# A hybrid recurrence and pooling decoder layer: heads by single levels among halves of projections, mean square in two fp32r passes, two meta queries directly, down projection in written order

## Chip, cores and metric

One core of a Trainium2 chip. The metric is the device time of one launch in microseconds (us). The engines are called PE (matrix unit), DVE (vector), ACT (scalar, activations), POOL (general purpose) and SP (which issues most transfers).

## The reference

One decoder layer over 1024 tokens of width 1024, with 16 learned meta tokens ahead of them, so L = 1040 rows, all in float32. Cut to what matters here:

```python
u = rmsnorm(h, mix_norm_pre)
q, f_logit, i_in, g_out, v_pool, gate_a, gate_b = split(u @ w_in)
a = hgrn2(q, f_logit, i_in, g_out, lb, out_gain)         # 4 heads of 128
p = multiscale_pool(v_pool, pool_proj, pool_scale)       # windows 2, 4, 8, 16
z = sigmoid(gate_a) * (a @ w_branch_hgrn) + sigmoid(gate_b) * (p @ w_branch_pool)
h = h + rmsnorm(z @ w_out, mix_norm_post)
u = rmsnorm(h, ffn_norm_pre)
gt = causal_dwconv(u @ ffn_w_gate, ffn_conv_w, ffn_conv_b)
y = (gelu(gt) * (u @ ffn_w_up)) @ ffn_w_down             # 2816 wide
h = h + rmsnorm(y, ffn_norm_post);  return h[:, N_META:]
```

Inside `hgrn2`, each head is a gated linear recurrence: with f = lb + (1 - lb) sigmoid(f_logit), b = cumsum(log f) and k = (1 - lb) sigmoid(-f_logit), the output at t is the sum over s <= t of (q_t exp(b_t - b_s) k_s) v_s. It is then divided by its root mean square over the 128 channels of the head, times a gain and sigmoid(g). Only the 1024 tokens leave the layer; of the 16 meta tokens the mixer needs outputs for the last two alone, since the convolution of width 3 looks two rows back.

## The kernel before

Everything lies with channels on the partitions and the 1040 rows along the free axis. A float32 product of full accuracy is made of three passes in fp32r, a rounded float32: each operand x is split into `xhi` (a cast by ACT) and `xlo` (the rest, by a subtraction), and hi*hi, hi*lo and lo*hi are added up in a bank of PSUM. A projection (`proj`) does this for 128 output channels: 8 blocks of k, three chunks of the rows (`CH_ALL`, 348 + 346 + 346 columns, or `CH_Q`, 3 x 342 for the last 1026 rows), one bank per chunk. The big products (gates, ffn, down projection) use Strassen's scheme.

The program runs through these stages (us of the profiled execution): projection of v up to 80; two early projections of the output gate g (heads 0 and 1, banks `pg`, made into `sg` by `post_g`) up to about 105, with the sums for the Strassen gates interleaved; the gates up to 250; the **head stage** from 250 to about 596; mixer output, ffn and, from about 1127, the down projection with its norm.

In the head stage the order is written in the string `ORDER`. A capital letter with a number is a projection for PE: F, Q, G for gate logit, query and output gate of a head, PV and PP for the pooling branch, BA and BB for the two branch products. `c` starts a head's chain on the logits (`chain_f`: clamps, logarithm, and the scan that gives b), `h2` is the next step of head 2, `sp`, `sa`, `w` are other small pieces. A scheduler then orders each engine's instructions from this program; so what stands on an engine follows from the written order and the scheduler's model.

A head's steps are the generator `head_steps`. The decayed scores within chunks of 128 are built by levels: for level lv = 2, 4, ..., 64 a block of 2 lv rows gives its second half's queries against its first half's keys, relative to the middle row. `level_in` makes `d`: a subtraction on b (L648), two exponentials on ACT, and the products with q (L652) and with kk (L653). `level_mm` multiplies on PE into `sl` (L668 with 64 columns, L664 for levels 32 and 64), and `level_out` copies the valid places into the score tile `sc`. Levels of 2, 4 and 8 also cover the meta tokens, with small matmuls into `sm` (L673) copied into `scm`. Then come the diagonal (`e1`, base, bank `sb`), the transposed keys `kt`, the sums of states over chunks (`ds`, added up by seven steps on DVE, L763), the outputs `po` from `sc` with v and from `qs` with the states (L780, L781; L773 for the meta rows), the square `rs` on ACT, and the mean square as a matmul with a matrix of 1/128 (`ms`, L788), plain fp32, one pass over three banks of 342 columns.

`POOLED` lists the operations that run on POOL instead of DVE: `sub` is the subtraction, `lq` and `lk` the products with q and kk, each with level and head; `w` a projection's weight split. `Loader` loads the weights of projections three ahead.

Steps of a head before, one per `h`: the inputs of levels 2 and 4; their matmuls and the inputs of 8 and 16; those and the inputs of 32 and 64; their matmuls, kd and e1; kt and base; ds; po and the square; ms.

The down projection runs in three stages of 11 steps (k). Each step's operands are loaded, cast (`rot`, L1496, ACT) and split (L1497, DVE) two steps ahead by `ahead`, and 24 matmuls into banks `pd` follow. For the last part, products `yh`, `yl` are prepared early from loads `yw` by `prep_last`.

Of the kernel before, what the change touches and what calls it, by code (L numbers as in the profile page):

```python
# [57 lines left out]
ORDER = ("F0 c0 Q0 h0 F1 h0 c1 Q1 h0 h1 F2 h1 c2 h0 Q2 h1 h2 G2 h0 h1 h2 h0 F3 h0 h2 c3 PV0 h1 h2 h1 Q3 h3 h1 h3 h1 "  # L58
         "PV1 h3 sp0 PV2 h2 h3 sa1 sp1 sp2 PP0 h2 PV3 h2 h3 sp3 PP1 h0 G3 w0 h3 PP2 h3 PP3 w1 BB0 w4 h2 BB1 w4 BB2 "
         "w4 sa2 BB3 w5 h3 BB4 w5 BB5 w5 sa0 sa3 BA0 BA1 w5 BB6 w2 BA2 w3 BB7 BA3 BA4 BA5 BA6 BA7")  # L60
POOLED = ("e1k.0 e1k.3 kdmul.2 kdmul.3 kdsub.2 lk32.1 lk4.1 lk64.0 lq16.1 lq16.3 lq32.0 lq32.1 lq32.2 lq4.0 "
          "lq64.0 lq64.3 lq8.0 lq8.1 lq8.2 osg.2 qsmul.2 qsmul.3 sub2.2 sub32.1 sub4.1 sub8.1 sub8.3 wBA2 wBA6 "
          "wBA7 wBB2 wF0 wF2 wF3 wPP2 wPV0 wPV1 wPV2 wPV3 wQ0 wQ1 wQ3").split()
# [7 lines left out]
def trunk_kernel(ctx: ExitStack, tc: tile.TileContext, x, meta_tokens, mix_norm_pre,  # L71
# [66 lines left out]
    pool_e.memset(onesm, 1.0 / P)  # L138

# [49 lines left out]
    def proj(w, col, n_k, xs, chunks, ws=None, name="pj", by_bank=0):  # L189
# [5 lines left out]
        for k in range(n_k - by_bank):  # L195
            for (lo, n), ps in zip(chunks, banks):
                xhi, xlo = xs(k, lo, n)
                pe.matmul(ps[:, :n], whi[:, k, :], xhi, start=(k == 0), stop=False)  # L198
                pe.matmul(ps[:, :n], whi[:, k, :], xlo, start=False, stop=False)  # L199
            for (lo, n), ps in zip(chunks, banks):  # L200
                xhi, _ = xs(k, lo, n)
                pe.matmul(ps[:, :n], wlo[:, k, :], xhi, start=False, stop=(k == n_k - 1))  # L202
# [3 lines left out]
        return banks  # L206
# [418 lines left out]
    def post_q(h, pq):  # L625
        q = slot(L, name="q")
        for (lo, n), ps in zip(CH_ALL, pq):
            act.copy(q[:, lo : lo + n], ps[:, :n])
        heads[h]["q"] = q

    def head_steps(h):
# [5 lines left out]
        scm = small([NM, NM], "scm", "scm", 2)  # L637
        pool_e.memset(sc, 0.0)
        pool_e.memset(scm, 0.0)


        def level_in(lv):
            lo = 0 if 2 * lv <= NM else NM
            nb = (L - lo) // (2 * lv)
            d = slot(L, name="d")
            bb, db = blocks(b, lo, lv), blocks(d, lo, lv)
            mid = bb[:, :, 0, lv - 1 : lv]
            eng(f"sub{lv}.{h}").tensor_tensor(db.rearrange("p b two h -> p b (two h)"), bb.rearrange("p b two h -> p b (two h)"),  # L648
                              mid.to_broadcast([P, nb, 2 * lv]), ALU.subtract)
            act.activation(db[:, :, 1, :], db[:, :, 1, :], AF.Exp)  # L650
            act.activation(db[:, :, 0, :], db[:, :, 0, :], AF.Exp, scale=-1.0)
            eng(f"lq{lv}.{h}").tensor_tensor(db[:, :, 1, :], db[:, :, 1, :], blocks(q, lo, lv)[:, :, 1, :], ALU.mult)  # L652
            eng(f"lk{lv}.{h}").tensor_tensor(db[:, :, 0, :], db[:, :, 0, :], blocks(kk, lo, lv)[:, :, 0, :], ALU.mult)  # L653
            return d

        def level_mm(lv, qk):
            ps = bank("sl")
            half = lv >= 32
            for c in range(NCH):
                t = NM + c * P  # L660
                if half:
                    for i in range(P // (2 * lv)):
                        s, n = t + 2 * lv * i, 2 * lv * i
                        pe.matmul(ps[n : n + lv, c * lv : (c + 1) * lv], qk[:, s : s + lv], qk[:, s + lv : s + 2 * lv],  # L664
                                  start=True, stop=True)
                    continue
                rhs = qk[:, t : t + P].rearrange("p (b two h) -> p b two h", two=2, h=lv)[:, :, 1, :]
                pe.matmul(ps[:, c * 64 : (c + 1) * 64], qk[:, t : t + P], rhs, start=True, stop=True)  # L668
            pm = None
            if 2 * lv <= NM:  # L670
                pm = bank("sm")
                rhs = qk[:, :NM].rearrange("p (b two h) -> p b two h", two=2, h=lv)[:, :, 1, :]
                pe.matmul(pm[:NM, : NM // 2], qk[:, :NM], rhs, start=True, stop=True)  # L673
            return ps, pm

        def level_out(lv, ps, pm):
# [12 lines left out]
            if pm is not None:  # L689
                dve.copy_predicated(scm.rearrange("p (b two h) -> p b two h", two=2, h=lv)[:, :, 1, :],  # L690
                                    masks[lv][:NM, : NM // 2].rearrange("p (b h) -> p b h", h=lv),
                                    pm[:NM, : NM // 2].rearrange("p (b h) -> p b h", h=lv))

        pend = []
        for pair in ((2, 4), (8, 16), (32, 64)):
            pend = [(lv, level_in(lv)) for lv in pair]
            yield
            outs = [(lv,) + level_mm(lv, d) for lv, d in pend]
            for o_ in outs:
                level_out(*o_)  # L700
# [3 lines left out]
        act.activation(qs, b, AF.Exp)  # L704
# [9 lines left out]
        eng(f"qsmul.{h}").tensor_tensor(qs, qs, q, ALU.mult)  # L714


        e1 = slot(L, name="e1")
        lo2 = lf.rearrange("p (b two) -> p b two", two=2)[:, :, 1]
        act.activation(e1[:, : L // 2], lo2, AF.Exp)
        act.activation(e1[:, L // 2 :], lo2, AF.Exp, scale=-1.0)  # L720
        q2 = q.rearrange("p (b two) -> p b two", two=2)[:, :, 1]
        k2 = kk.rearrange("p (b two) -> p b two", two=2)[:, :, 1]
        eng(f"e1q.{h}").tensor_tensor(q2, q2, e1[:, : L // 2], ALU.mult)
        eng(f"e1k.{h}").tensor_tensor(k2, k2, e1[:, L // 2 :], ALU.mult)
# [11 lines left out]
        act.copy(ktm, pm[:NM, :P])  # L736
        for j in range(2):
# [7 lines left out]
        pm = bank("sm")  # L745
        pe.matmul(pm[:NM, :NM], kk[:, :NM], q[:, :NM], start=True, stop=True)
        dve.copy_predicated(scm, mbase[:NM, :NM], pm[:NM, :NM])
# [25 lines left out]
        pe.matmul(pm[:, :NM], vmeta[:NM, h * P : (h + 1) * P], scm, start=True, stop=True)  # L773
        act.copy(o[:, :HALO], pm[:, T0:NM])
# [9 lines left out]
        act.activation(rs, o, AF.Square)  # L784
        yield
        for lo, n in CH_Q:
            ps = bank("ms")
            pe.matmul(ps[:, :n], onesm, rs[:, lo : lo + n], start=True, stop=True)  # L788
# [49 lines left out]
    def split(src, name):  # L838
        hi, lo_ = slot(TQ, F32R, name + "h"), slot(TQ, F32R, name + "l")
        act.copy(hi, src)  # L840
        dve.tensor_tensor(lo_, src, rr(hi), ALU.subtract)
# [180 lines left out]
    with tc.manual_schedule(engines={E.Activation, E.DVE, E.PE}):  # L1022
# [88 lines left out]
    jobs_ = [o_ for o_ in order if o_[0].isupper()]  # L1111
# [21 lines left out]
    gens, after = {}, {}  # L1133
    for kind, i in order:
# [12 lines left out]
        if kind == "h":  # L1147
# [3 lines left out]
            continue  # L1151
        src, n_k, xs, chunks, post = job(kind, i)
        if kind in ("BA", "BB"):
            load_gate(sas if kind == "BA" else sbs, kind == "BB", i)
        ws = loader.next()
        if (kind, i) == ("BA", KD - 1):
            z0 = [split_z(0, k) for k in range(ZA)]
        banks = proj(None, 0, n_k, xs, chunks, ws=ws, name="p" + kind.lower(),
# [513 lines left out]
    ahead(1)  # L1672
    for s_ in range(3):
        banks = [[bank("pd") for _ in range(NT)] for _ in range(2)]
        for k in range(KH):
            at = s_ * KH + k
            for b_, o_ in zip(banks, preps.pop(at)):
                multiply(b_, o_, k == 0, k == KH - 1)
            ahead(at + 2)
            if s_ == 2 and k in (1, 2):  # L1680
                for t in range(NT):
                    c = (c21, c12)[k - 1][t]
                    dve.tensor_tensor(c, c, u2[t], ALU.subtract)
            if at >= 3 and early and at % 3 == 0:
                load_ops(3, early[0][0])
            if at >= 3 and early and at % 3 == 2:
                prep_last(*early.pop(0))
            if s_ == 2 and k in (KH - 6, KH - 4):
                for t in ((0, 1) if k == KH - 6 else (2, 3)):
                    load_h(NT + t)  # L1690
            if s_ == 2 and k == KH - 3:
                load_ops(3, KH - 2)
                load_ops(3, KH - 1)
        pa, pb = banks
        for t in range(NT):
# [6 lines left out]
            else:  # L1702
                dve.scalar_tensor_tensor(c22[t], c12[t], -1.0, pa[t], ALU.mult, ALU.subtract)
                dve.tensor_tensor(c21[t], c21[t], pa[t], ALU.add)

# [51 lines left out]
```

## Time and profile before

| | |
|---|---|
| time, median of 3 runs | 1345.61 us (1345.18 to 1348.58) |
| profiled execution | 1347.15 us, span 1345.4 |
| mean granted clock of PE | 0.995 |
| PE busy | 1328.6 us, 99% |
| DVE, ACT, POOL busy | 72%, 42%, 33% |

A row of a timeline reads: start, duration, engine, line, operation, out<-in, sizes, xcount, and in brackets the idle time before it with what ended it. A group row has count, busy time and mean ns. A row of windows has from:to, length, busy time of each engine with its count, then PE's granted clock as a share, the share of DMA, and GB/s. A row that names a tile gives min/median/max ns.

### The profile page before, as it was taken

What the parts mean: (1) busy time and instruction counts of PE and PEld (TensorE: products, weight loads), DVE (VectorE), ACT (ScalarE), POOL (GpSimd) and SP (SyncE); (2) the same over time, 40 slices, a digit from 0 to 9 for tenths busy, and PEclk for the clock granted to TensorE, in tenths of its full rate; (3) what the DMA queues carried; (4) which work ended last, traced back from release to release, by engine and by line L of the source; (5) the groups of instructions that cost most, each with busy time, mean ns of one, the idle gap of its engine ahead of it and who ended that gap; (6) DMA issues with size and microseconds to landing.
All of it is one profiled execution on the core that took longest, in us unless ns stands there. A gap on an engine that the chain in (4) does not pass through costs nothing.

```text
span 1345.4 us, 19942 instructions
## 1 busy us (share of the span) xinstructions
PE 1328.6 (99%) x7721; PEld 1183.5 (88%) x7721; DVE 972.1 (72%) x1236; ACT 563.7 (42%) x935; POOL 438.1 (33%) x327
## 2 busy tenths in 40 slices
PE   8999999999999999999999999999999999999997
PEld 7799999999999999987889888888888888788886
DVE  6754644389865957776668999889889886644657
ACT  6543333366464465224565322222222223543443
POOL 2015421236442610033016556446456652000000
PEclk9999999998999999999999999999999999999999
DMA  7134333311110138886686777775667799966624
GB/s 269 42 112 155 118 118 107 106 48 48 34 50 19 33 100 305 277 310 222 233 317 223 223 204 203 204 204 149 169 154 154 189 231 308 372 203 194 194 95 157
DMA packets 139665, 230.38 MB, mean 171 GB/s; under 512 B 9000, under 2 KB 77196, under 8 KB 139570
## 3 DMA queue, kind: packets, MB, share of 16 engines
q1 hardware_dynamic: 127506, 204.71, 45.1%
q0 software_dynamic: 12064, 24.38, 10.9%
q8 instruction: 61, 1.00, 0.3%
q14 instruction: 34, 0.28, 0.1%
HBM read 165.56 MB, written 86.53 MB: 187 GB/s over the span
## 4 chain that ended last, share of the span: by engine, by line
PE 86%; DVE 6%; DMA 4%; issue 2%; ACT 2%; SPq 0%; DVEq 0%; ACTq 0%
PE P L301 15%; PE P L302 14%; PE P L304 14%; PE pd L185 5%; PE pd L186 5%; PE pd L187 5%; PE pm L185 2%; PE pm L187 2%; PE pm L186 2%; PE sl L668 2%; PE pq L198 1%; PE pv L186 1%; PE pq L202 1%; PE pq L199 1%; PE pv L187 1%
## 5 line engine op out<-in xcount | busy, mean ns | idle before, releaser
L302 PE MATMUL P<-v,whi 128*128 128x512 f32 (+2 forms) x408 | 140.7, 353 | 0.0
L301 PE MATMUL P<-v,whi 128*128 128x512 f32 (+2 forms) x408 | 140.7, 352 | 0.0
L304 PE MATMUL P<-v,wlo 128*128 128x512 f32 (+2 forms) x424 | 135.1, 349 | 0.0
L187 PE MATMUL pd<-rot 128*128 128x512 f32 x272 | 105.8, 389 | 0.0
L186 PE MATMUL pd<-rot 128*128 128x512 f32 x272 | 105.8, 389 | 0.0
L1497 DVE TENSOR_TENSOR rot<-yt,rot 128x1024 fp32r<-128x1024 f32 x33 | 40.3, 1222 | 67.7 <-ACT rot L1496 67.7
L272 POOL TENSOR_TENSOR swa<-wraw,wraw 128x512 f32<-128x512 f32 x28 | 42.2, 1506 | 136.1 <-DMA wraw<-in_ffn_w_gate_dram 72.2
L301 PEld LDWEIGHTS P<-v,whi 128*128 128x128 f32 x408 | 76.7, 188 | 10.4
L302 PEld LDWEIGHTS P<-v,whi 128*128 128x128 f32 x408 | 76.6, 188 | 10.2
L304 PEld LDWEIGHTS P<-v,wlo 128*128 128x128 f32 x424 | 74.0, 188 | 10.8
L246 ACT CAST whi<-wraw 128x512 fp32r<-128x512 f32 x78 | 46.1, 618 | 86.0 <-PE P L302 62.6
L185 PE MATMUL pd<-rot 128*128 128x512 f32 x272 | 72.4, 390 | 0.9 <-ACT rot L1496 0.8
L1496 ACT CAST rot<-yt 128x1024 fp32r<-128x1024 f32 x33 | 34.6, 1053 | 83.7 <-PE pd L186 83.5
L246 ACT CAST whi<-swa 128x512 fp32r<-128x512 f32 x56 | 33.4, 619 | 81.6 <-PE P L302 78.8
L247 DVE TENSOR_TENSOR wlo<-swb,whi 128x512 fp32r<-128x512 f32 x56 | 62.9, 1129 | 6.2 <-ACT whi L246 6.2
L247 DVE TENSOR_TENSOR wlo<-wraw,whi 128x512 fp32r<-128x512 f32 x74 | 63.3, 877 | 3.0 <-ACT whi L246 3.0
L1425 DVE SCALAR_TENSOR_TENSOR y<-g,par,y 128x1024 f32<-128x1024 f32 x44 | 64.7, 1470 | 0.8
L246 ACT CAST whi<-swb 128x512 fp32r<-128x512 f32 x56 | 33.4, 619 | 70.4 <-PE P L302 66.0
L185 PEld LDWEIGHTS pd<-rot 128*128 128x128 f32 x272 | 50.9, 188 | 12.6 <-ACT rot L1496 1.6
L187 PEld LDWEIGHTS pd<-rot 128*128 128x128 f32 x272 | 51.1, 188 | 10.6
L186 PEld LDWEIGHTS pd<-rot 128*128 128x128 f32 x272 | 51.1, 188 | 10.6
L301 PE MATMUL P<-t4h,whi 128*128 128x258 f32 (+1 forms) x196 | 57.0, 307 | 0.0
(408 smaller groups left out, 4136.7 us busy)
## 6 DMA issues: line engine op xcount, KB each, us to landing
wraw<-in_w_in_dram SPq DMA_DIRECT2D x36, 512.0 KB, 4.3
yt<-ysum SPq DMA_DIRECT2D x33, 512.0 KB, 4.1
wraw<-in_ffn_w_gate_dram SPq DMA_DIRECT2D x26, 512.0 KB, 7.9
wraw<-in_ffn_w_up_dram SPq DMA_DIRECT2D x22, 512.0 KB, 5.6
wsum<-in_ffn_w_down_dram SPq DMA_DIRECT2D x22, 512.0 KB, 8.9
wraw<-in_w_out_dram SPq DMA_DIRECT2D x18, 512.0 KB, 4.8
ysum<-ys SPq DMA_DIRECT2D x11, 768.0 KB, 8.4
sa<-sscr SPq DMA_DIRECT2D x16, 513.0 KB, 5.8
```

Of the source, the lines that this page charges most:

```text
L185: pe.matmul(ps, ahi, bhi, start=first, stop=False)
L186: pe.matmul(ps, ahi, blo, start=False, stop=False)
L187: pe.matmul(ps, alo, bhi, start=False, stop=last)
L246: act.copy(hi, src)
L247: (pool_e if 4 <= i < 2 * self.early else dve).tensor_tensor(lo, src, rr(hi), ALU.subtract)
L272: pool_e.tensor_tensor(s1, a21, a22, ALU.add)
L301: pe.matmul(d, whi[:, k, :], xh[:, c : c + w], start=(k == 0 and onto is None), stop=False, **go)
L302: pe.matmul(d, whi[:, k, :], xl[:, c : c + w], start=False, stop=False, **go)
L304: pe.matmul(x[:, o : o + w], wlo[:, k, :], xh[:, c : c + w], start=False, stop=(k == 3), **go)
L1425: dve.scalar_tensor_tensor(a, g[:, j : j + SEQ], cvw[:, j, m : m + 1], a, ALU.mult, ALU.add)
L1496: act.copy(hi, src)
L1497: dve.tensor_tensor(lo, src, rr(hi), ALU.subtract)
```

## The change

`head_steps` goes from eight to twelve steps: after the inputs of a pair of levels, each level's matmuls and copies are a step of their own, and kt, base and so on are apart: inputs 2, 4 and meta; meta and level 2; level 4, inputs 8, 16; level 8; level 16, inputs 32, 64; level 32; level 64, kd, e1; kt; base; ds; po, square and split; ms. `ORDER` is new, and some projections stand in it as halves (`Qa2` and `Qb2`): `proj_parts` yields after half of the blocks of k, and the banks stay held in between. Operations change between DVE and POOL:

```diff
-ORDER = ("F0 c0 Q0 h0 F1 h0 c1 Q1 h0 h1 F2 h1 c2 h0 Q2 h1 h2 G2 h0 h1 h2 h0 F3 h0 h2 c3 PV0 h1 h2 h1 Q3 h3 h1 h3 h1 "
+ORDER = ("F0 c0 Q0 h0 F1 h0 h0 c1 Q1 h0 h1 h0 F2 h1 h1 c2 h0 h0 Qa2 Qb2 h1 h1 h2 G2 h0 h0 h1 Fa3 h1 h2 h0 h2 Fb3 "
...
```

In `POOLED`, to DVE go lk64.0, lq16.3, lq32.0, lq4.0, qsmul.3, sub4.1, sub8.3, wPV2, wPV3 and wQ3; to POOL go e1q.1, e1q.3, kdsub.1, lk32.0, lk32.3, lq2.1, lq4.3, lq64.1, qsmul.1, rsl.0, sub2.3 and wQ2.

The levels no longer cover the meta rows. The scores of the two meta queries that are needed are made directly: their decay factors `em` (2 x 16 columns), then two tiny matmuls into `sm`, and two into `po`. The Q projection covers 1026 columns.

```diff
+        def meta_in():
+            e3 = em.rearrange("p (i t) -> p i t", i=HALO)
+            last = b[:, T0:NM].rearrange("p (i o) -> p i o", o=1).to_broadcast([P, HALO, NM])
+            dve.tensor_tensor(e3, last, over(b), ALU.subtract)
+            act.activation(em, em, AF.Exp)
+            dve.tensor_tensor(e3, e3, over(kk), ALU.mult)
+
+        def meta_mm():
+            pm = bank("sm")
+            for i in range(HALO):
+                pe.matmul(pm[:NM, i * HALO : (i + 1) * HALO], em[:, i * NM : (i + 1) * NM], q[:, T0:NM], start=True,
+                          stop=True)
+            act.copy(scm, pm[:NM, : 2 * HALO])
...
         def level_in(lv):
-            lo = 0 if 2 * lv <= NM else NM
+            lo = NM
...
-        pe.matmul(pm[:, :NM], vmeta[:NM, h * P : (h + 1) * P], scm, start=True, stop=True)
-        act.copy(o[:, :HALO], pm[:, T0:NM])
+        for i in range(HALO):
+            n = T0 + i + 1
+            pe.matmul(pm[:, i * HALO : (i + 1) * HALO], vmeta[:n, h * P : (h + 1) * P], scm[:n, i * HALO : (i + 1) * HALO],
+                      start=True, stop=True)
+        act.copy(o[:, :HALO], pm[:, : 2 * HALO : HALO + 1])
...
         act.activation(rs, o, AF.Square)
+        rh, rl = split(rs, "r", eng(f"rsl.{h}"))
         yield
         for lo, n in CH_Q:
             ps = bank("ms")
-            pe.matmul(ps[:, :n], onesm, rs[:, lo : lo + n], start=True, stop=True)
+            pe.matmul(ps[:, :n], onesr, rh[:, lo : lo + n], start=True, stop=False)
+            pe.matmul(ps[:, :n], onesr, rl[:, lo : lo + n], start=False, stop=True)
...
-            return (wblock(WIN, 0, KD, CQ + i * P, P), KD, u_all, CH_ALL, lambda r: post_q(i, r))
+            return (wblock(WIN, 0, KD, CQ + i * P, P), KD, u_q, CH_Q, lambda r: post_q(i, r))
```

The second early gate projection finishes its banks one after the other (`by_bank=2` for the last two blocks of k), and its `post` stands ahead of the sums:

```diff
-            r = proj(None, 0, n_k, xs, chunks, ws=gl.next(), name="pg")
+            r = proj(None, 0, n_k, xs, chunks, ws=gl.next(), name="pg", by_bank=2 * h)
+            if h == EARLY_G - 1:
+                post(r)
             for j in SUMS_AT.get(9 + 2 * h, ()):
                 next(sums[j], None)
-            post(r)
+            if h < EARLY_G - 1:
+                post(r)
```

In the down projection ACT and DVE keep the written order, and a stage's banks are evicted (`leave`) right behind the last step's matmuls, ahead of the next preparation:

```diff
+    with tc.manual_schedule(engines={E.Activation, E.DVE}):
...
+                if k == KH - 1:
+                    pa, pb = banks
+                    leave(s_, pa, pb)
+                ahead(at + 2)
-            ahead(at + 2)
```

What the orders of the engines show. First DVE, from the scan of head 1 (`b_2832` before, `b_2837` after) to the product with kk of its level 2 (`d_3014` before, `d_2992` after), with head 0's levels 32 and 64 (`d_2996`, `d_3002` before; `d_3017`, `d_3023` after). Before:

```order
L622 SCALAR_TENSOR_TENSOR b_2832<-keep_on_2526,f_2833 128x1040
L648 TENSOR_TENSOR d_2996<-b_2629 128x1024
L648 TENSOR_TENSOR d_3002<-b_2629 128x1024
L648 TENSOR_TENSOR d_3014<-b_2832 128x1040
L152 TENSOR_TENSOR wlo_2966<-wraw_2963,whi_2965 128x1024
L688 COPY_PREDICATED sc_2734<-mask_149,sl_2973 128x64x8
L690 COPY_PREDICATED scm_2735<-mask_149,sm_2982 16x8
L653 TENSOR_TENSOR d_2996<-d_2996,kk_2628 128x16x32
L652 TENSOR_TENSOR d_3020<-d_3020,q_2969 128x130x4
L688 COPY_PREDICATED sc_2734<-mask_154,sl_2984 128x32x16
L652 TENSOR_TENSOR d_3014<-d_3014,q_2969 128x260x2
L653 TENSOR_TENSOR d_3014<-d_3014,kk_2831 128x260x2
```

The same place after:

```order
L632 SCALAR_TENSOR_TENSOR b_2837<-keep_on_2528,f_2838 128x1040
L656 TENSOR_TENSOR em_2990<-b_2837 128x32
L658 TENSOR_TENSOR em_2990<-em_2990,kk_2836 128x32
L675 TENSOR_TENSOR d_2992<-b_2837 128x1024
L675 TENSOR_TENSOR d_2998<-b_2837 128x1024
L675 TENSOR_TENSOR d_3017<-b_2631 128x1024
L675 TENSOR_TENSOR d_3023<-b_2631 128x1024
L155 TENSOR_TENSOR wlo_2969<-wraw_2966,whi_2968 128x1024
L710 COPY_PREDICATED sc_2736<-mask_151,sl_2976 128x64x8
L680 TENSOR_TENSOR d_2992<-d_2992,kk_2836 128x256x2
```

Level 4's subtraction (`d_2998`) has come to DVE, and its product with q, level 32's product and a copy now stand behind; level 2's product with q has gone to POOL.

Second PE, from the end of head 1's second chunk of `po` to the next projection, with levels 2 and 4 of head 3 (`d_4002`, `d_4008` before; `d_3920`, `d_3926` after). Before, this `po` follows the projection Q3 directly:

```order
L668 MATMUL sl_4042<-d_4002 128x64 x8
L673 MATMUL sm_4051<-d_4002 16x8
L668 MATMUL sl_4053<-d_4008 128x64 x8
L673 MATMUL sm_4062<-d_4008 16x8
L788 MATMUL ms_4080<-rs_4015,onesm 128x342
L198 MATMUL ppv_4092<-uhi_86,whi_3642 128x348
```

After, where state sums (`ds`) of head 1 and `po` of heads 0 and 1 stand between Q3 and these rows; the `st` of the last `po` is head 1's:

```order
L803 MATMUL po_3986<-qs_3529,st_3894 128x128
L691 MATMUL sl_4001<-d_3681 32x32 x16
L663 MATMUL sm_4020<-q_3890,em_3918 16x2 x2
L695 MATMUL sl_4024<-d_3920 128x64 x8
L691 MATMUL sl_4034<-d_3687 64x64 x8
L695 MATMUL sl_4059<-d_3926 128x64 x8
L811 MATMUL ms_4081<-rh_3997,onesr 128x342
L208 MATMUL ppv_4096<-uhi_88,whi_3638 128x348
```

Levels 32 and 64 of head 2 (`d_3681`, `d_3687`) have come in between, and the passes of `ms` with rl follow later, behind 13 matmuls of ppv.

Third ACT at the beginning of the down projection, with the casts of `yw`. Before:

```order
L1496 CAST rot_10512<-wd_10414 128x1024
L1496 CAST yh_10782<-yw_10713 128x1024
L1496 CAST yh_10886<-yw_10819 128x1024
L1496 CAST rot_10512<-yt_10418 128x1024
L1496 CAST rot_10512<-wd_10419 128x1024
L1496 CAST yh_11005<-yw_10922 128x1024
```

After:

```order
L1534 CAST rot_10526<-wraw_10721 128x1024
L1534 CAST rot_10526<-yt_10720 128x1024
L1534 CAST yh_10798<-yw_10729 128x1024
L1534 CAST rot_10526<-wraw_10757 128x1024
L1534 CAST rot_10526<-yt_10756 128x1024
```

The first cast of `yw` has moved from the first steps to the sixth, and the others follow one in three steps.

More of the change, by code (lines that the diff above doesn't have):

```diff
@@ L187, in mm3, with proj, proj_parts @@
         pe.matmul(ps, alo, bhi, start=False, stop=last)
-    def proj(w, col, n_k, xs, chunks, ws=None, name="pj", by_bank=0):
+    def proj(*a, **k):
+        for banks in proj_parts(*a, **k):
+            pass
+        return banks
+    def proj_parts(w, col, n_k, xs, chunks, ws=None, name="pj", by_bank=0):
         if ws is None:
@@ L626, in post_q @@
         q = slot(L, name="q")
[L627 to L628 removed]
+        for (lo, n), ps in zip(CH_Q, pq):
+            act.copy(q[:, T0 + lo : T0 + lo + n], ps[:, :n])
         heads[h]["q"] = q
@@ L668, in level_mm, with level_out @@
                 pe.matmul(ps[:, c * 64 : (c + 1) * 64], qk[:, t : t + P], rhs, start=True, stop=True)
[L669 to L676, printed above, removed]
+            return ps
+        def level_out(lv, ps):
             if lv >= 32:
@@ L1151, in trunk_kernel @@
             continue
+        kind, part = kind.rstrip("ab"), kind[-1]
         src, n_k, xs, chunks, post = job(kind, i)
+        if part == "b":
+            banks = next(halves_of[kind, i])
+            loader.ahead()
+            pay()
+            after[kind, i] = post(banks)
+            continue
         if kind in ("BA", "BB"):
@@ L1671, in trunk_kernel, with leave @@
     early = [(k, True) for k in list(range(KT, KH - 2)) + list(range(KT))]
[L1672 to L1678, printed above, removed]
-            ahead(at + 2)
[L1680 to L1694, printed above, removed]
+    def leave(s_, pa, pb):
         for t in range(NT):
```

89 lines of the change are left out of this document (57 added, 32 removed), and 3 rows, old and new, of the table ORDER.

## Prediction

> **What bounds the kernel now.** I read the page first, then the waits of TensorE (PE), then windows of the head stage, then the timelines of PE and VectorE (DVE) around the two places that the windows showed.
>
> ```profile
> span 1345.4 us, 19942 instructions
> PE 1328.6 (99%) x7721; PEld 1183.5 (88%) x7721; DVE 972.1 (72%) x1236; ACT 563.7 (42%) x935; POOL 438.1 (33%) x327
> PE pba L198 <- DVE sa L872: 1.8, 3, 1.3
> PE sl L668 <- DVE d L653: 1.7, 2, 0.9
> PE pd L185 <- ACT rot L1496: 0.8, 1, 0.8
> PE po L773 <- DVE plo L848: 0.8, 1, 0.8
> PE P L301 <- ACT sg L801: 0.7, 1, 0.7
> ```
>
> PE is busy in 1328.6 of 1345.4 us, so all its waits together are 16.8 us; five of them, above, lie in what the change touches. The rest of any gain has to be less matmul work or a faster clock. The windows show that the clock is not always full:
>
> ```profile
> 300.00:330.00 30.00, 29.89 (x29) 0.89 0.19 53
> ...
> 310.00:320.00 10.00, 9.05 (x84) 8.49 (x84) 10.00 (x12) 8.47 (x14) 5.98 (x3) 0.74 0.19 54
> 320.00:330.00 10.00, 10.00 (x68) 9.88 (x67) 9.89 (x11) 6.49 (x7) 5.42 (x5) 0.92 0.19 52
> 410.00:420.00 10.00, 9.26 (x65) 7.83 (x63) 9.40 (x12) 7.60 (x12) 3.42 (x2) 0.86 0.18 52
> 420.00:430.00 10.00, 10.00 (x62) 9.77 (x61) 3.02 (x3) 3.47 (x5) 0.00 (x0) 0.97 0.00 0
> ```
>
> The first row is DVE alone: 29.89 busy of 30 us, so here a later DVE is a later PE. In the others the columns are PE, weight loads, DVE, ScalarE (ACT), GpSimd (POOL), and then PE's granted clock: 0.74 and 0.92, 0.86 and 0.97, where it is 1.00 all around. The clock lost is 10 x (0.26 + 0.08) = 3.4 us at the first place and 10 x (0.14 + 0.03) = 1.7 us at the second, 5.1 together. The timeline of PE shows what stands there:
>
> ```profile
> 312.84 2.00 PE L668 MATMUL sl<-d 128*128 128x64 f32 x16 [0.95 <-DVE d L653]
> 314.92 3.68 PE L668 MATMUL sl<-d 128*128 128x64 f32 x16
> 414.96 2.00 PE L668 MATMUL sl<-d 128*128 128x64 f32 x16 [0.74 <-DVE d L653]
> 417.03 3.65 PE L788 MATMUL ms<-rs,onesm 128*128 128x342 f32 x6
> 315.00:317.00 2.00, 2.00 (x10) 0.50 0.34 89
> 345.00:353.00 8.00, 8.00 (x98) 1.00 0.04 10
> 468.00:476.00 8.00, 7.91 (x66) 1.00 0.23 66
> 467.90 0.39 PE L773 MATMUL po<-scm,vmeta 16*128 16x16 f32 x2 [0.80 <-DVE plo L848]
> 472.12 1.04 PE L731 MATMUL pt<-ident,kd 128*128 128x128 f32 x8
> ```
>
> Both times PE first waits, 0.95 and 0.74 us, for the product of a level (d, L653); 2 us later the clock is at 0.50, and the same 16 matmuls of a level that take 2.00 us take 3.68. Small matmuls without a wait do not do this (345 to 353: 1.00), nor does a wait of 0.80 ahead of small po matmuls (468 to 476: 1.00). So the pattern is a wait of 0.7 us or more ahead of the 64-column sl matmuls, and each costs itself plus 1.7 to 3.4 us of clock.
>
> [...]
>
> **The change part by part: PE's own work.**
>
> ```profile
> 476.64 1.89 PE L788 MATMUL ms<-rs,onesm 128*128 128x342 f32 x6
> 478.52 0.32 PE L199 MATMUL pg<-ulo,whi 128*128 128x342 f32 x1
> 478.68 0.32 PE L202 MATMUL pg<-uhi,wlo 128*128 128x342 f32 x1
> 298.24 0.21 PE L673 MATMUL sm<-d 128*16 128x8 f32 x2
> 298.38 0.43 PE L668 MATMUL sl<-d 128*128 128x64 f32 x2
> ```
>
> Mean square: three plain fp32 banks hold PE from 476.64 until the second pg starts at 478.52, less one pg (0.16 from start to start): 1.72 us, 0.57 a bank. Two fp32r passes cost 2 x 0.16 = 0.32. Twelve banks save 12 x 0.25 = 3.0 us. Q projections: 1040 columns become 1026, so 14 x 8 x 3 x 4 = 1344 columns less, at 0.16 / 342 us each: 0.6 us.
>
> Meta queries: gone are 12 sm of the levels (0.14 from start to next start), 4 sm of the base (taken as the same) and 4 po of scm (0.39, the row at 467.90): 16 x 0.14 + 4 x 0.39 = 3.8 us. New are 8 sm and 8 po of two columns. If all cost as an sm does, 16 x 0.14 = 2.2; if the po stay at 0.39, 1.1 + 3.1 = 4.2. So between -1.6 and +0.4; I take -0.6, the middle, since the matrices are smaller than either row's. PE's work: -3.0 - 0.6 - 0.6 = -4.2 us.
>
> **The two waits of the head stage.** DVE before the first:
>
> ```profile
> 297.71 6.32 DVE L648 TENSOR_TENSOR d<-b 128x1024 f32<-128x1024 f32 x3
> 303.96 2.33 DVE L152 TENSOR_TENSOR wlo<-wraw,whi 128x1024 fp32r<-128x1024 f32 x1
> 306.88 1.11 DVE L653 TENSOR_TENSOR d<-d,kk 128x512 f32<-128x512 f32 x1
> 307.91 1.79 DVE L652 TENSOR_TENSOR d<-d,q 128x520 f32<-128x520 f32 x1
> 309.62 0.72 DVE L688 COPY_PREDICATED sc<-mask,sl 128x512 f32<-128x512 uint8 x1
> 310.24 1.94 DVE L652 TENSOR_TENSOR d<-d,q 128x520 f32<-128x520 f32 x1
> 312.10 0.69 DVE L653 TENSOR_TENSOR d<-d,kk 128x520 f32<-128x520 f32 x1
> ...
> L652 POOL TENSOR_TENSOR d<-d,q x11: 1281/1727/3544, 275.7 to 441.8; 128x512 f32<-128x512 f32 x7, 128x520 f32<-128x520 f32 x4
> L648 DVE TENSOR_TENSOR d<-b x19: 1199/1228/3446, 270.4 to 438.1; 128x1024 f32<-128x1024 f32 x11, 128x1040 f32<-128x1040 f32 x8
> ```
>
> The product that PE waits for ends at 312.79. In the new order DVE does ahead of it, after the scan of head 1, one subtraction more (four for three) and two small em operations, but no longer the level-32 product, the two multiplications by q and one copy (1.11 + 1.79 + 1.94 + 0.72 = 5.6 us); the multiplication by q of level 2 is now POOL's and runs beside. With subtractions at the 2.1 us that they take here this makes +2.1 + 0.3 - 5.6 = -3.2; with their undisturbed 1.2 the four take 4.9 instead of the three's 6.3, and it is -6.7. PE arrives less than 1 us sooner (some 0.6 of the savings above come ahead of it). So 3.2 to 6.7 earlier stands against a wait of 0.95: it goes, with 3.4 of clock. What is late next is level 4 and then 32, whose last products are now POOL's (1.7 each, one behind the other), two matmul groups of 2 us later.
>
> At the second, Q3 is now followed by the state sums of head 1 and by po of heads 0 and 1 before the levels of head 3, where it was po of one head alone. Sixteen more pairs of small matmuls (a po of 4.2 us, 467.90 to 472.12 in the rows above) stand ahead of the product that was 0.74 late: it goes, with 1.7 of clock. New there is a chain: po of head 1 reads states that DVE sums seven times (0.35 each) among five level operations; the first half is due 4.2 us after ds, the rest up to 8.4 after. Undisturbed the chain takes 7 x 0.35 + 1.2 + 4 x 0.69 = 6.4 us, so it just fits; disturbed it is 2 to 4 us late.
>
> ```profile
> L763 DVE SCALAR_TENSOR_TENSOR st<-st,ebl,ds x28: 328/347/348, 363.5 to 497.5; 128x128 f32<-128x128 f32 x28
> L784 ACT ACTIVATE rs<-o x4: 1059/1060/1064, 375.9 to 501.4; 128x1026 f32<-128x1026 f32 x4
> ```
>
> **Where the costs are hidden.** The split of rs adds an ACT pass (1.06) and a subtraction (1.2) between po and ms, and the rl pass of the first ms stands behind 13 wide matmuls in PE's order; I cost it at nothing, and at up to 2.3 us a head if that cover is gone. DVE loses the sixteen copies of scm; the swaps between DVE and POOL nearly cancel. Split projections ask for the next weights half a projection later; DMA share is 0.2 or less in the rows of 300 to 430 above, so nothing.
>
> **Ends of other stages.** The early gate's 0.7 us (P behind sg) goes, since head 1's banks now finish one after the other and are drained ahead of the sums. In the down projection the 0.81 us go: the casts of yw that ACT did early, each behind its load, stood ahead of rot:
>
> ```profile
> 1141.11 1.05 ACT L1496 CAST yh<-yw 128x1024 fp32r<-128x1024 f32 x1 [6.03 <-DMA yw<-in_ffn_w_down_dram]
> 1150.66 2.11 PE L185 MATMUL pd<-rot 128*128 128x512 f32 x8 [0.81 <-ACT rot L1496]
> L1497 DVE TENSOR_TENSOR rot<-yt,rot 128x1024 fp32r<-128x1024 f32 x33 | 40.3, 1222 | 67.7 <-ACT rot L1496 67.7
> ```
>
> Written order puts one such cast among three steps. Its danger is a late load with rot queued behind it; a step's two casts (1.05) and two subtractions (1.22) are 4.5 us if nothing overlaps, and PE waits for them nowhere else in the stage (0.8 is all of that wait). I take -0.7, bounds -0.8 and +3 (half of the 6.03 wait reaching PE once).
>
> **Sum.** -4.2 (work) - 1.7 (two waits) - 5.1 (clock) - 0.7 - 0.7 = -12.4. Against it stand new waits, which no row of before shows. Their bounds are 0 and +9 (the two waits with their clock, 6.8, once again, and 2.3 for ms). I take what the late part of the stage has now (0.80 + 1.8, which I leave unchanged) as the size of what a new order meets afresh, 2.6, plus one short loss of clock, 1.7: +4.3. So -8.1 us: 1347.15 - 8.1 = 1339.0 for an execution like the profiled one. That one is 1.5 above the median of 1345.61, so I give 1337.5. About 0.3%, 4 us, is what a measurement of this kernel can tell from no change.
>
> **Rivals.** (1) The waits move instead of going: level 4 or 32 of the same group is late, and the clock falls there. For it: POOL has two products in a row there. Then 6.8 isn't gained, and the +1.7 is already in it: 1337.5 + 6.8 - 1.7 = 1342.6. (2) The half clock belongs to the sl matmuls and not to the wait. For it: both places are sl; against it: 345 to 353. Then the waits go and 5.1 of clock stay, of which the sum has 1.7 already: 1337.5 + 5.1 - 1.7 = 1340.9, and up to 3.4 more if the new, longer groups are slowed throughout; 1342 between. [...] (3) Slower: DVE becomes the bound in 300 to 430. In the first two heads POOL gets seven operations and gives three: four multiplications at 1.7 and three on whole rows, twice the columns, at an estimated 2 x 1.28 (the least of that POOL row) = 2.6, less two and one of these: 8.6 us more. Beside POOL a multiplication on DVE takes up to 1.94 for 0.69 and a subtraction 2.1 for 1.2: about half of POOL's time is lost to DVE, 4.6 us, and DVE has no room (29.89 of 30). PE then waits 4.6 more, with another 3.4 of clock, and neither old wait goes: -4.2 - 1.4 + 2.6 + 4.6 + 3.4 = +5.0, so 1350.6. It decides from 3.6 us of lateness on. Against it: the seven take 6.4 us off DVE itself, the three bring back 2.6. (4) The two fp32r passes cost as much as plain fp32: 3.0 more, 1340.5; the pg rows speak against it.
>
> **Chances.** Forecast 0.66 (own range 1332 to 1342), rival 1 0.14, rival 2 0.08, rival 3 0.08, rival 4 0.04. Low end: new waits at 0 and the rest as summed, 1345.6 - 12.4 = 1333.2, and 1.2 for the meta and DVE bounds: 1332. High end: rivals 1 and 2 with 1.5 for the down projection, 1344. Outside lie rival 3 and a tenth of the rest. Faster than 1341.6: 0.62 of the forecast, rival 4 and a third of rivals 1 and 2, 0.74. Slower than 1349.6: rival 3, 0.08. Same: 0.18.
>
> **What would show it.** Right: no row of half clock at the two places, ms banks of 0.32 us, no wait of pd for rot, P for sg gone, PE busy about 8 us less. Wrong: a window under 0.9 in the head stage between 300 and 430, sl or po waiting over 1 us for d or st, or ms waiting for rl.

## The result, and the profile after

The changed kernel takes 1330.03 us (median of 4 runs, 1330.01 to 1330.10) against 1345.39 for the kernel before (median of 4, 1340.95 to 1348.58) on the same chip: ratio 0.9888, 95% interval 0.986 to 0.9916. That is 15.4 us faster where 8.1 were forecast, and below the low end of the range, 1332. In the experiments below the kernel before ran some fifty times more and had medians of 1344.0 to 1344.4, so the gain is 14 to 15 us. The profiled execution took 1330.10, 17.05 less than the one of before, 1347.15, which lies at the slow end of that kernel's runs. The experiments ran on three chips, each with the kernel before beside them; a difference from the changed kernel is taken from 1330.03 and so compares across chips, on which the kernel before differs by 0.4 us. (One run of before in the experiments, 1741.68 us at a granted clock of 0.764, and one of `work_only`, 2197.77 us at 0.555, are left out of the comparisons.)

The page of the changed kernel, and the five longest waits of PE:

```profile
span 1328.4 us, 19923 instructions
PE 1317.1 (99%) x7713; PEld 1177.6 (89%) x7713; DVE 970.7 (73%) x1229; ACT 566.8 (43%) x946; POOL 440.4 (33%) x327
...
PE pj L507 <- POOL ident masks.py:199: 1.5, 1, 1.5
PE pv L188 <- ACT uhi L434: 0.8, 1, 0.8
PE pt L431 <- DVE un L420: 0.8, 1, 0.8
PE pv L189 <- DVE wlo L517: 0.5, 2, 0.3
PE sl L691 <- ACT sg L825: 0.4, 1, 0.4
```

All five waits that the prediction quoted are gone: sl for d, pba for sa, pd for rot, po for plo, P for sg. One of 0.4 us is new (the last row); the other four are at the program's start, as before. Ten-us windows of the head stage after:

```profile
310.00:320.00 10.00, 10.00 (x113) 9.59 (x112) 10.00 (x10) 9.30 (x15) 5.75 (x4) 1.00 0.37 107
320.00:330.00 10.00, 10.00 (x74) 10.00 (x72) 9.71 (x12) 5.79 (x7) 4.55 (x3) 1.00 0.01 2
340.00:350.00 10.00, 9.56 (x97) 9.32 (x96) 9.90 (x10) 9.67 (x16) 7.20 (x5) 1.00 0.18 54
410.00:420.00 10.00, 10.00 (x67) 10.00 (x66) 8.91 (x7) 8.26 (x12) 8.79 (x4) 1.00 0.00 0
```

PE is busy all through them except for the 0.44 us in 340 to 350, and the clock is 1.00 in every window of the stage, those not shown too. The group that stood at half clock, and DVE ahead of it:

```profile
310.50 3.79 PE L695 MATMUL sl<-d 128*128 128x64 f32 x32
314.21 1.77 PE L691 MATMUL sl<-d 128*32 128x32 f32 x48
304.75 1.18 DVE L680 TENSOR_TENSOR d<-d,kk 128x512 f32<-128x512 f32 x1
```

The level-2 product is done at 305.93 and PE takes it at 310.50: 4.6 us of slack where there were 0.95 of wait, and levels 2, 4, 32 and 64 follow without a gap. Before, the two groups of 16 and the matmuls of levels 32 and 64 behind them had taken 2.00, 3.68 and 2.94 us.

The head stage (first pf to first pm) is 335.1 us long after 350.1, the stages ahead of it 0.5 shorter, the mixer output and ffn 0.1 and the down projection 1.4. So nearly the whole gain is the head stage's.

### The profile page after: what moved, and what is told of

Read it like the earlier page. It is cut to its first block, busy times and chain, and to the rows that moved or that the text cites. A ratio compares the mean times of both kernels' runs of the same rounds, so it can differ in the third digit from the quotient of the medians.

```text
span 1328.4 us, 19923 instructions
## 1 busy us (share of the span) xinstructions
PE 1317.1 (99%) x7713; PEld 1177.6 (89%) x7713; DVE 970.7 (73%) x1229; ACT 566.8 (43%) x946; POOL 440.4 (33%) x327
## 3 DMA queue, kind: packets, MB, share of 16 engines
q0 software_dynamic: 12064, 24.38, 10.8%
## 4 chain that ended last, share of the span: by engine, by line
PE 95%; DVE 4%; DMA 0%; ACT 0%; issue 0%; SPq 0%; DVEq 0%
PE P L311 15%; PE P L312 15%; PE P L314 15%; PE pd L188 5%; PE pd L190 5%; PE pd L189 5%; PE pm L188 2%; PE pm L189 2%; PE pm L190 2%; PE sl L695 1%; PE ppv L208 1%; PE pbb L208 1%; PE ppv L212 1%; PE pbb L209 1%; PE ppv L209 1%; PE pbb L212 1%
## 5 line engine op out<-in xcount | busy, mean ns | idle before, releaser
L1535 DVE TENSOR_TENSOR rot<-wraw,rot 128x1024 fp32r<-128x1024 f32 x31 | 38.0, 1225 | 72.3 <-ACT rot L1534 72.2
L312 PEld LDWEIGHTS P<-v,whi 128*128 128x128 f32 x408 | 76.6, 188 | 10.2
L314 PEld LDWEIGHTS P<-v,wlo 128*128 128x128 f32 x424 | 74.0, 188 | 10.8
L190 PE MATMUL pd<-rot 128*128 128x512 f32 x272 | 82.1, 389 | 0.0
L189 PE MATMUL pd<-rot 128*128 128x512 f32 x272 | 82.1, 389 | 0.0
L188 PE MATMUL pd<-rot 128*128 128x512 f32 x272 | 81.1, 389 | 0.1
L1534 ACT CAST rot<-wraw 128x1024 fp32r<-128x1024 f32 x31 | 32.7, 1055 | 90.8 <-PE pd L190 89.4
L257 DVE TENSOR_TENSOR wlo<-swb,whi 128x512 fp32r<-128x512 f32 x56 | 59.9, 1075 | 6.9 <-ACT whi L256 6.9
```

The source lines that it names most:

```text
L188: pe.matmul(ps, ahi, bhi, start=first, stop=False)
L189: pe.matmul(ps, ahi, blo, start=False, stop=False)
L190: pe.matmul(ps, alo, bhi, start=False, stop=last)
L257: (pool_e if 4 <= i < 2 * self.early else dve).tensor_tensor(lo, src, rr(hi), ALU.subtract)
L312: pe.matmul(d, whi[:, k, :], xl[:, c : c + w], start=False, stop=False, **go)
L314: pe.matmul(x[:, o : o + w], wlo[:, k, :], xh[:, c : c + w], start=False, stop=(k == 3), **go)
```

## The experiments

**Work and order apart.** Two kernels take the change into halves. `order_only` is the changed kernel with the work of before; `work_only` is the kernel before with the new work. With the first line of the diff go the matmuls into sm and the copies into scm, with the last the split of rs. Other lines of the same parts are left out here.

```diff
 order_only, against the changed kernel
-            lo = NM
+            lo = 0 if 2 * lv <= NM else NM
...
-KD, u_q, CH_Q, lambda r: post_q(i, r))
+KD, u_all, CH_ALL, lambda r: post_q(i, r))
...
-            pe.matmul(ps[:, :n], onesr, rh[:, lo : lo + n], start=True, stop=False)
-            pe.matmul(ps[:, :n], onesr, rl[:, lo : lo + n], start=False, stop=True)
+            pe.matmul(ps[:, :n], onesm, rs[:, lo : lo + n], start=True, stop=True)
 work_only, against the kernel before: the same lines the other way round
```

> The changed kernel with the work of before: levels over the meta rows with sm, scm copies and the base sm, 1040 columns of Q, plain fp32 mean square. New order, halves, swaps between the engines, early gate and down projection stay. Theory A (work and order add): the two waits for d, their half clock and the late waits for sa and plo stay away, so 1345.4 - 3.9 (waits) - 5.1 (clock) - 1.8 (early gate and down projection) = 1334.6. Theory B (the waits went because DVE and ScalarE lost work): sl waits for d again by 0.5 us or more at one place at least, with half clock, 1340 or more.

> The kernel before with the new work alone: two meta queries directly, Q over 1026 columns, mean square in two fp32r passes; order, steps, swaps, early gate and down projection of before. Theory A: PE has 4.2 us less by the prediction's prices (5.9 by the difference of the two traces in the head stage), the two waits for d and the half clock stay: 1339.5 to 1341. Theory B: no wait for d and no half clock, 1335 or less.

Measured: `order_only` 1339.67 us (ratio to before 0.9969, 0.9955 to 0.9983), `work_only` 1346.72 (1.002, 1.0009 to 1.0031). Both theories miss. The order with the old work gains 4, the work with the old order loses 3, and both together gain 14. Waits of `order_only`, then waits and windows of `work_only`:

```profile
PE pf L206 <- DVE sc L751: 1.9, 1, 1.9
PE sm L755 <- DVE sc L751: 0.6, 1, 0.6
```

```profile
PE sl L687 <- DVE d L672: 4.0, 1, 4.0
PE ppv L200 <- ACT st L762: 2.4, 1, 2.4
...
306.03 1.27 DVE L650 TENSOR_TENSOR em<-em,kk 128x32 f32<-128x32 f32 x1
308.97 2.50 DVE L671 TENSOR_TENSOR d<-d,q 128x512 f32<-128x512 f32 x1
...
310.00:320.00 10.00, 5.95 (x33) 0.67 0.18 52
320.00:330.00 10.00, 10.00 (x84) 0.64 0.20 54
```

In the old order the new work puts a small operation (em, 1.27 us here) ahead of the level products on DVE and the multiplications by q meet POOL (2.50 each, where 0.69 is their median in the kernel before); the wait for d grows from 0.95 to 4.05, and the half clock behind it comes to 10 x (0.33 + 0.36) = 6.9 us, 0.8 of them while PE still waited. PE's work did shrink, and waits and clock took all of it back: with the waits taken out and half clock counted at half, the matmuls of the head stage take 334.0 us, and 340.3 in the kernel before. In the new order the old work brings two other waits, 2.5 together, and 6.4 us more of PE work (head stage 343.4 instead of 335.1, less 1.9 more of waits; 341.0 against 334.5). So the new work is worth 6.4 us in either order, where 4.2 were priced.

**The ends alone.** The kernel before with the early gate and the down projection of the changed one.

```diff
+            r = proj(None, 0, n_k, xs, chunks, ws=gl.next(), name="pg", by_bank=2 * h)
...
+    with tc.manual_schedule(engines={E.Activation, E.DVE}):
```

> The kernel before with only the early gate (second projection bank by bank, its post ahead of the sums) and the down projection in written order. Theory A: 0.5 to 0.7 us at the gate and 1.3 at the down projection, 1343.5, no wait of pd for rot. Rival: the transfers of yw, spread over the stage, make rot late elsewhere and give the 0.8 back: 1344.5 to 1346.

Measured: 1342.1 us, ratio 0.9984 (0.9972 to 0.9996). In the trace the head stage begins at 245.9 instead of 246.4 and the down projection takes 216.8 instead of 218.1: 0.5 + 1.4 = 1.9 us, theory A. No wait of P for sg or of pd for rot is left. This run also showed something else. Its waits and a window:

```profile
PE sl L668 <- DVE d L653: 1.7, 2, 1.0
410.00:420.00 10.00, 9.26 (x70) 1.00 0.12 35
```

The two waits for d are still there, but at the second the clock stays at 1.00, where the same 0.74 us had been followed by 1.7 us of lost clock.

**The mean square alone.** The changed kernel with the plain fp32 pass (the last three lines of the first diff) and without the split of rs.

> The changed kernel with the mean square as one plain fp32 pass again, no split of rs. Theory A (0.25 us a bank, as priced): 1330.0 + 3.0 = 1333.0. Rival (the term was undersized, since plain fp32 among wide matmuls costs more than its own rows): 1334.5 or more. Second rival: without the split the order of DVE and ScalarE shifts and a new wait comes, seen in the waits of PE.

Measured: 1337.41 us, 7.4 more than the changed kernel; the profiled execution is 6.6 longer. I summed, for every matmul of the head stage, the time from its start to the next start without the waits: ms 5.39 us instead of 3.88, and the wide matmuls that follow a bank of ms (pbb, pg, ppv) 1.69 more, 3.2 in all. So the price of 3.0 was right, and the second rival is true as well: of the other 3.4, 2.5 are waits and 0.8 is lost on pba, where PE starts again behind them. The longest wait is this one, among wide matmuls:

```profile
564.71 0.42 PE L206 MATMUL pba<-ah,whi 128*128 128x342 f32 x1 [2.09 <-ACT whi L162]
```

**What a wait does to the clock.** `wait_10` and `wait_13` put copies in place on ACT behind the level-2 product of head 1 in the changed kernel; `sl_five` issues the same level's matmuls five times without a wait.

```diff
+            if lv == 2 and h == 1:
+                for _ in range(10):                    # 13
+                    act.copy(db[:, :, 0, :], db[:, :, 0, :])
...
 sl_five
+                for _ in range(5 if h == 1 and lv == 2 else 1):
```

> The changed kernel with ten copies in place on ScalarE behind the level-2 product of head 1, which was ready 4.6 us before PE took it: 5.3 us of copies, so PE waits some 0.8 us ahead of the sl matmuls, as it did before the change. Theory W (a wait together with the light sl matmuls drops the clock, and by chance from one execution to the next): 1330.8 without and up to 1336 with half clock, and a spread over several us between runs of the one program, where the changed kernel spread over 0.1. [...]

> The same with thirteen copies: PE waits 2.4 us ahead of the sl matmuls. Theory W: half clock in most executions, on this group of 5.6 us of small matmuls up to the next projection, 1332.4 + 3 to 6 = 1335.5 to 1338. [...]

> The changed kernel with each level-2 matmul of head 1 issued five times into the same place: 32 matmuls more at 0.24 us, a group of 13 us of small matmuls and no wait. Theory W: clock 1.00 and 1330 + 7.7 = 1337.7. Rival 2 of the prediction (the sl matmuls themselves bring the half clock): windows at 0.5 from 314 on and 1344 or more.

Measured: `wait_10` 1335.32 us (1334.63 to 1336.38), `wait_13` 1346.92, `sl_five` 1337.34. The waits came out longer than meant, 2.43 and 12.20 us: a copy took 0.69 us where 0.53 had been reckoned, and in `wait_13` the last two copies came behind other work of ACT. Timeline and windows of `wait_10`, of `wait_13`, and of `sl_five`:

```profile
313.06 6.26 PE L698 MATMUL sl<-d 128*128 128x64 f32 x32 [2.43 <-ACT d L683]
319.26 2.97 PE L694 MATMUL sl<-d 128*32 128x32 f32 x48
310.00:320.00 10.00, 7.57 (x67) 0.70 0.19 54
320.00:330.00 10.00, 10.00 (x73) 0.79 0.20 52
```

```profile
322.85 7.06 PE L698 MATMUL sl<-d 128*128 128x64 f32 x32 [12.20 <-ACT d L683]
329.84 2.97 PE L694 MATMUL sl<-d 128*32 128x32 f32 x48
...
312.00:314.00 2.00, 0.00 (x0) 0.63 0.00 0
330.00:332.00 2.00, 2.00 (x43) 0.50 0.00 0
332.00:334.00 2.00, 2.00 (x15) 0.75 0.84 254
334.00:336.00 2.00, 2.00 (x15) 1.00 0.03 8
```

```profile
310.52 10.93 PE L696 MATMUL sl<-d 128*128 128x64 f32 x96
321.38 1.77 PE L691 MATMUL sl<-d 128*32 128x32 f32 x48
310.00:320.00 10.00, 10.00 (x92) 1.00 0.19 54
320.00:330.00 10.00, 10.00 (x105) 1.00 0.19 54
```

12.6 us of small matmuls without a wait keep the clock at 1.00, so rival 2 of the prediction falls. After a wait the 64-column ones do not bring it back: in `wait_13` the clock falls about 2 us into the wait (PE is idle from 310.65 on, and 0.63 over 312 to 314 is half speed from 312.5) and stays at 0.50 through ten us of sl. It returns at 333.0 (0.75 over 332 to 334), 0.3 us after the first wide matmul has started at 332.74; which of the matmuls brought it back is not shown. The last section comes back to this. In `wait_10` a wait of 2.43 us is followed by 10 x (0.30 + 0.21) = 5.1 us of lost clock: the two small groups take 6.26 and 2.97 instead of 3.79 and 1.77, the rest falls on the projection behind them. Its profiled span is 6.3 us longer than the changed kernel's.

**The same kernel once more.** The kernel before, unchanged, profiled in one more execution.

> The kernel before, unchanged, profiled once more. Theory W (whether a wait of 0.7 to 1 us drops the clock is chance): the same waits for d at 312 and 415 within 0.1 us, but at least one of the two stretches of half clock missing or of another length, and a time that differs by that. Rival (the half clock belongs to this code): 0.74 and 0.86 in the two windows again, 1347 us.

Measured: 1344.54 us. Timeline and windows:

```profile
312.99 2.00 PE L668 MATMUL sl<-d 128*128 128x64 f32 x16 [0.95 <-DVE d L653]
310.00:320.00 10.00, 9.05 (x105) 1.00 0.19 55
350.00:360.00 10.00, 9.41 (x64) 0.83 0.16 53
410.00:420.00 10.00, 9.26 (x61) 0.85 0.13 38
```

The wait of 0.95 is there to the hundredth, and this time the clock holds; it falls at 350 instead, behind waits of 0.32 and 0.27, and again at 414. So theory W: the wait is in the code, whether it costs clock differs from one execution to the next. Runs of this kernel spread over 1340.7 to 1348.6, in the experiments with a mean clock of 0.999 and 0.998 in the fastest (1340.7, 1340.9) and 0.994 to 0.995 in the slowest (1347.3, 1347.6). The changed kernel, with no wait over 0.44 us in its head stage, spread over 0.1.

**The swaps.** `pooled_old` is the changed kernel with the list `POOLED` of before, `subs_pool` with two subtractions alone put back.

```diff
 subs_pool
...
-          "lk32.0 e1q.3 e1q.1 lq2.1 wQ2 sub2.3 rsl.0 lk32.3 lq64.1 qsmul.2").split()
+          "lk32.0 sub4.1 sub8.3 e1q.3 e1q.1 lq2.1 wQ2 sub2.3 rsl.0 lk32.3 lq64.1 qsmul.2").split()
```

> The changed kernel with the old list of operations on POOL. Theory A (the swaps keep POOL and VectorE from meeting where VectorE is full): waits of sl for d or of PE for copies come back, 0.5 to 4 us with clock, 1332 to 1338. Rival (steps and order alone do it): 1330 to 1331.

> The changed kernel with two subtractions back on POOL: level 4 of head 1 (ahead of the sl group at 310) and level 8 of head 3 (ahead of the one near 420). With the whole old list PE waited 1.95 and 3.06 us for d at these two. Theory A (these two of the twenty-two swaps carry it): waits of 1 to 3 us at both places, with half clock in most executions, 1334 to 1342. Rival (the whole balance, not single operations): no wait over 0.5 us, 1330 to 1331.

Measured: `pooled_old` 1342.41 us, `subs_pool` 1336.14 (1335.75 to 1336.96). Waits and windows of the first, then of the second:

```profile
PE sl L695 <- DVE d L680: 3.1, 1, 3.1
PE sl L695 <- DVE d L679: 2.0, 1, 2.0
310.00:320.00 10.00, 8.05 (x90) 0.83 0.18 54
420.00:430.00 10.00, 6.94 (x43) 0.94 0.00 0
430.00:440.00 10.00, 10.00 (x46) 0.55 0.03 8
```

```profile
PE sl L695 <- DVE d L680: 1.6, 1, 1.6
420.00:430.00 10.00, 8.36 (x54) 0.86 0.03 8
430.00:440.00 10.00, 10.00 (x53) 0.80 0.00 0
```

With the old list 12 us of the gain are gone. The profiled execution shows 5.0 of waits and 10 x (0.17 + 0.06 + 0.45) = 6.8 of clock (its span is 10.8 longer). The prediction had put the swaps at nothing ("nearly cancel"). Level 8's subtraction of head 3 accounts for half of it: put back with level 4's of head 1, it brings 1.64 us of wait and 3.4 of clock near 425. Level 4's brings no wait at 310; theory A holds at one place and its rival at the other.

**The tail.** The order of before from BB1 on.

```diff
-BB0 w4 h2 w4 BB1 BB2 BB4 w5 h3 BB3 w4 h3 w5 sa2 BB5 w5 sa0 BB7 sa3 BA0 w5 BB6 w2 BA2 w3 BA4 BA1 BA5 BA6 BA3 BA7
+BB0 w4 h2 BB1 w4 BB2 h3 w4 sa2 BB3 w5 h3 BB4 w5 BB5 w5 sa0 sa3 BA0 BA1 w5 BB6 w2 BA2 w3 BB7 BA3 BA4 BA5 BA6 BA7
```

> The changed kernel with the order of before from the second branch projection (BB1) on. Theory A (the late waits for sa and whi went because the branch projections were reordered): pba waits 1 to 2.5 us again among wide matmuls, clock 1.00 there, 1331 to 1332.5. Rival (they went because head 3 was done earlier and DVE was freer there): 1330.0 to 1330.5.

Measured: 1333.88 us (1332.67 to 1335.24), 3.9 more. Waits and windows:

```profile
PE pbb L208 <- ACT rs L813: 1.8, 1, 1.8
PE pm L188 <- DVE sa L896: 0.7, 1, 0.7
510.00:520.00 10.00, 8.20 (x49) 0.96 0.92 313
520.00:530.00 10.00, 10.00 (x57) 0.87 0.96 319
```

So the old order of the branch projections brings late waits, as theory A has it, though the time lies above its range, they stand at other places than expected, and one of them, ahead of wide matmuls, also lost 10 x (0.04 + 0.13) = 1.7 us of clock.

**Q.** The changed kernel with Q over 1040 columns.

> The changed kernel with Q over 1040 columns again. The prediction priced this at 0.6 us; against the run with all old work the pq matmuls differed by 1.15 (0.1569 to 0.1609 us each). Expected: 1330.0 + 1.15 = 1331.2 if no wait comes with it, 1330.6 by the prediction's price; the occupancy of pq in the trace decides.

Measured: 1331.22 us in two runs (1330.41 and 1332.04). The pq matmuls take 46.13 us from start to start instead of 45.19, so 0.94; the profiled execution shows only 0.3 more, because the 0.44 us at 345 did not come. The price of 0.6 was too low.

## Why the prediction was wrong

The bottleneck and the cause of the two old waits for d were read rightly; two steps failed, both in the sum, and PE's work and some small terms were too low. The prediction's terms, and what the traces before and after show (us; the rows on matmuls are start-to-start times in the head stage, waits taken out and half clock counted at half):

| term | predicted | traces |
|---|---|---|
| clock at the two places | -5.1 | -5.1 |
| two waits for d | -1.7 | -1.7 |
| mean square | -3.0 | -2.7 (3.2 in `ms_plain`) |
| Q | -0.6 | -1.05 |
| meta queries (sm 1.2, sl 0.8, sb 0.5 less, po 1.2 more) | -0.6 | -1.4 |
| early gate | -0.7 | -0.5 |
| down projection | -0.7 | -1.4 |
| late waits for plo and sa (0.80, 1.8, 0.35) | 0 | -2.95 |
| pba, which starts again behind four pauses | none | -1.0 |
| other matmuls, mixer output and ffn | none | +0.3 |
| new waits and their clock | +4.3 | +0.6 |
| sum | -8.1 | -16.9 (measured -17.05) |

**"I take what the late part of the stage has now [...] as the size of what a new order meets afresh, 2.6, plus one short loss of clock, 1.7: +4.3."** This is the step that failed most, by 3.7 us: one wait of 0.44 came. The price was a habit, not a reading. The order of the new program was at hand, and the slack at each place follows from it as it did for the first wait (there "3.2 to 6.7 earlier" turned into 5.5: 4.6 of slack instead of 0.95 of wait). The experiments show that the figure is a fair one for an order that does not fit its work: 2.5 us of waits in `order_only`, 2.5 new ones in `ms_plain`, 5.0 and 6.8 of clock in `pooled_old`, 8.3 and 8.6 in `work_only`. Each is the changed kernel or the one before with one part exchanged, and each came out slower than the priced terms of that part make it. Order, list and work fit one another, and the prediction, which priced them one by one, left that out.

**"... which I leave unchanged".** The waits for plo and sa went too, 2.95 us. The prediction had quoted the rows of both and did not work out their places in the new order. `tail_old` ties late waits, and 3.9 us, to the order of the branch projections. It says nothing of plo, whose wait of 0.80 stood at 468, ahead of the part that it exchanges; what removed that one was not tried apart.

**PE's work and the small terms.** PE's work was put at -4.2, and the two pairs of kernels with equal order, 340.3 and 334.0, 341.0 and 334.5, show 6.4. The prediction counted the sm and po matmuls alone, while the sl and sb between which the sm stood became cheaper too, and Q gave 1.05 where 0.6 were priced. A wait costs more than its bracket, which the prediction took as the whole: in the trace before, pba starts at 565.88 and again at 567.49, 1.61 apart, with a wait of 1.28 between, where two starts otherwise lie 0.16 apart, so 0.17 more; the next start follows 0.26 later instead of 0.16. With four such places pba took 1.0 us more. The down projection gave 1.4 instead of 0.7: the prediction took only the wait, and kept no account of the other rows of that stage.

**What held.** Both old waits for d went by the mechanism described. The 0.3 us for the two em operations of head 1 was an estimate from no row of before; in the trace after they take 0.19 each (295.44 and 295.93). The chain of seven state sums under the two po took 5.9 us (395.89 to 401.83), priced 6.4, and just fitted:

```profile
395.89 0.73 DVE L782 SCALAR_TENSOR_TENSOR st<-st,ebl,ds 128x128 f32<-128x128 f32 x2 [1.23 <-PE ds L779]
401.50 0.33 DVE L782 SCALAR_TENSOR_TENSOR st<-st,ebl,ds 128x128 f32<-128x128 f32 x1
```

The passes of ms start 0.15 to 0.16 apart among the wide matmuls, as the pg rows had said, and rival 4 falls:

```profile
488.10 0.32 PE L811 MATMUL ms<-rh,onesr 128*128 128x342 f32 x1
488.25 0.32 PE L812 MATMUL ms<-rl,onesr 128*128 128x342 f32 x1
```

Rivals 1 and 3 did not come, but `work_only` looks like rival 3: DVE late beside POOL, and slower by 0.2%.

**The clock.** The full 5.1 us is right for the profiled execution, and too much for the median, which was taken from it by subtracting 1.5: the kernel before loses clock in some executions more than in others, and its runs with a mean clock of 0.999 take 1341 to 1343. Against those the change brings 11 to 13 us. So the match of the 5.1 in the table is that of the one execution on which it was priced, and luck as far as the median goes.

## What to carry to other kernels

When an order is replaced as a whole, work out the slack at every place where the engine at the limit waited, and at those where it now might, from the new order; do not price the unknown places by the old kernel's waits. Parts of such a change can't be priced one by one: here work alone lost 3 us, order alone gained 4, both 14. A kernel whose runs spread by half a per cent, as the kernel before did here (1340.7 to 1348.6 us), may be losing clock behind short waits; look at the granted clock in fine windows before taking one profile as typical.

## What the runs showed of the hardware

The half clock comes in pieces. Lost clock in the head stage, summed over windows as above, was 3.4 and 1.7 us in the kernel before, 1.7 and 1.7 when it was profiled again, 5.1 in `wait_10`, 10.2 in `wait_13`, 6.9 and 1.7 in `work_only`, 1.7 and 5.1 in `pooled_old`, 3.4 in `subs_pool` and in `ends_only`, 1.7 in `tail_old`: to 0.1 us always a multiple of 1.7, that is of 3.4 us at half speed. In the trace before, windows of 0.2 us put the two stretches of half clock at 314.8 to 321.6 and 417.2 to 420.6, so 6.8 and 3.4 us long. What sets these lengths is not shown.

The length of the wait alone does not say whether the clock falls. It fell behind waits of 0.95 and 0.74 us in the kernel before, and behind 0.32 with 0.27 when it was profiled again, where small matmuls stood around them, and behind 2.44 (`work_only`, ppv) and 1.8 (`tail_old`, pbb) ahead of wide ones. In `wait_13` it fell 2 us after PE went idle. It did not fall behind the 0.95 when the kernel before was profiled again, nor behind the 0.74 in `ends_only`, nor behind 1.86 us (`order_only`, pf) and 2.09 (`ms_plain`, pba), these two again among wide ones.

What tells these cases apart is not shown: no run varied the matmuls around a wait with its length held. The 64-column matmuls hold the full clock where they follow without a wait (10.93 us of them in `sl_five`, at 1.00), and behind a wait that has brought the half clock they run on at 0.50 (7.06 us of them in `wait_13`). The clock returned 0.3 us after the first wide matmul behind them had started in `wait_13`, 2.0 after it in `wait_10` (324.16 after 322.16) and 2.1 in `work_only` (327.12 after 325.06). A wait ahead of a long group of 64-column matmuls can cost nearly the whole group at half speed: the 32 of them that take 3.79 us in the changed kernel took 6.26 in `wait_10`, 7.06 in `wait_13` and 7.09 in `work_only`.

Whether single levels as steps and projections in halves, apart from the order and the list, carry part of the gain was not tried.
